# Up projection of a two-layer trunk: high weights times high and low activations as one 512-column product, halves added at eviction, and one ring of four PSUM banks

## The chip, the cores and the metric

The kernel runs on one core of a Trainium2 chip (trn2). The metric is device time in microseconds (us) from start to end of one execution. TensorE (PE) does the matrix products and writes them to PSUM, which has 8 banks of 128 partitions x 2 KB; VectorE (DVE), ScalarE (ACT) and GpSimd (POOL) work on tiles in SBUF and read or write PSUM; SyncE (SP) issues the transfers from HBM. Each engine works through its own program in order and waits on semaphores for the others.

## The reference

Two layers on x of 256 tokens x 1024 channels in fp32. Each layer is FFN, mixer, FFN, each with a norm before and a norm after; the mixer of layer 0 is a causal convolution of width 31, that of layer 1 an HGRN2 recurrence.

```python
def swiglu_ffn(x, w_in, w_out):                  # w_in 1024 x 5632, w_out 2816 x 1024
    gate, up = jnp.split(x @ w_in, 2, axis=-1)
    return (jax.nn.silu(gate) * up) @ w_out

for layer in range(2):
    g = norm_gains[layer]
    h = swiglu_ffn(rms_norm(x, g[0]), ffn_w_in[layer, 0], ffn_w_out[layer, 0])
    x = x + 0.5 * rms_norm(h, g[1])
    hn = rms_norm(x, g[2])
    m = conformer_conv_module(hn, ...) if layer == 0 else hgrn2_mixer(hn, ...)
    x = x + rms_norm(m, g[3])
    h = swiglu_ffn(rms_norm(x, g[4]), ffn_w_in[layer, 1], ffn_w_out[layer, 1])
    x = x + 0.5 * rms_norm(h, g[5])
```

The convolution module is: project to 2048 channels, `a * sigmoid(gate)`, depthwise convolution, layer norm, silu, project back. HGRN2 projects to queries q, forget gates f, values and output gates, and scans the tokens with a decaying state.

## The kernel before

**Precision.** Every fp32 operand of a large product is split into a high and a low part (`split`, L130 to L132: ACT casts to fp32r, DVE subtracts), and a product is three: high x high, high x low, low x high. The activations' parts are `xth` and `xtl`, [channel, token], made by `pre_norm` (PE transposes at L168, ACT L172, DVE L178).

**Weights.** `weight` streams 328 tiles of 512 KB through a ring of four raw tiles; high and low parts (`wh`, `wl`) have rings of ten.

**FFN** (`ffn`). The 2816 hidden channels are eleven chunks `c` of 256. Chunk 0 goes token-major by `project`, for which the activations are the stationary operand and the weights 512 moving columns (L242, L243, and for the low activations L246). The other ten go channel-major by `up_both` and `channels`: a call of `channels` makes gate and up of 128 hidden channels for all 256 tokens, with a 128x128 weight block stationary and 256 tokens moving, 3 products for each of 8 k, for gate and for up, 48 in all (L281, L282, L283), into the two halves of one PSUM bank. One DVE multiply by the tokens' scales brings it to SBUF (L286); ACT Sigmoid L334, two DVE multiplies and a `split` make the hidden parts, which `down` multiplies with `w_out` (`expand`, `mm3`, L135 to L137) into four accumulator banks (`acc`). There are 80 such calls in the four FFNs and 8 in HGRN.

**Conv mixer** (200 to 275 us). For each token tile t and chunk c: `gate` (a `project`, then DVE L396, ACT L399, DVE L401 and a split into `lg`), then `conv`: the products u from `lg` (a Fourier transform, L135 to L137 into a bank `tr`), DVE L421 to L425 and a split into `cc`, then the products v back, from `cc`. Eight (t, c) in all.

**HGRN scores** (711 to 790 us). For each half: `channels` calls for f and q, then `scores`: eight products L547, a multiply of q by f (L550), and seven levels in a chain: eight products L562 into a bank `tr` (each shows as two records in the trace), DVE `copy_predicated` L568 (a copy L565 in the last level), DVE multiply of q (L573), POOL L577 and L579; then X at L624.

**Between the parts.** `start` (L290 on) runs the `pre_norm` of tile 0, then `rest` of the part before (the last down products and `post_norm` of tile 1), then the `pre_norm` of tile 1. `post_norm` is ACT L212, DVE L213, POOL L146 and L148, DVE L218, which writes `x`.

**What sets the order.** The kernel is written in the order above; the framework that builds it places each engine's instructions by priority as their inputs and buffers come free, so that products of one step stand between those of another. The eight PSUM banks are three rings: `acc` 4, `mm` 2 (`project`, `channels`) and `tr` 2 (transposes, u, v, scores, X).

Of the kernel before, what the change touches and what calls it, by code (L numbers as in the profile page):

```python
# [8 lines left out]
F32 = mybir.dt.float32  # L9
F32R = mybir.dt.float32r  # L10
U8 = mybir.dt.uint8
AF = mybir.ActivationFunctionType
ALU = mybir.AluOpType
# [3 lines left out]
P = 128  # L17
D = 1024
ROOT = 32.0
KD = D // P  # L20
# [3 lines left out]
SEQ = 256  # L24
NT = SEQ // P
# [15 lines left out]
def trunk_kernel(  # L41
# [14 lines left out]
    act, dve, pool, pe = nc.scalar, nc.vector, nc.gpsimd, nc.tensor  # L56

    const = ctx.enter_context(tc.tile_pool(name="const", bufs=1))
    sb = ctx.enter_context(tc.tile_pool(name="sb", bufs=2))
    ps = ctx.enter_context(tc.tile_pool(name="ps", bufs=2, space=PSUM))  # L60
# [3 lines left out]
    def new(pl, shape, dtype, tag, bufs):  # L64
        count[0] += 1
        return pl.tile(shape, dtype, tag=tag, name=f"{tag}_{count[0]}", bufs=bufs)

    def b4(dtype=F32):
        return new(sb, [P, 1024], dtype, "b4", 10)

    def wide(tag, dtype=F32):
        return new(sb, [P, 512], dtype, tag, {"ga": 2, "lg": 5, "ca": 2, "cb": 2, "cc": 4}[tag])

    def narrow(tag, dtype=F32):
        return new(sb, [P, 256], dtype, tag, {"e": 4, "hid": 4}[tag])

    def tiny(n=1):
        return new(sb, [P, 16], F32, "tiny", 16)[:, :n]
# [1 line left out]
    def acc():  # L80
        return new(ps, [P, 512], F32, "acc", 4)

    def mm():
        return new(ps, [P, 512], F32, "mm", 2)

    def tr():
        return new(ps, [P, 512], F32, "tr", 2)

    ident = const.tile([P, P], F32, name="ident")
    make_identity(nc, ident)  # L90
# [5 lines left out]
    pool.memset(ones, 1.0)  # L96

    xs = [const.tile([P, D], F32, name=f"x{t}") for t in range(NT)]
    xth = const.tile([P, NT * D], F32R, name="xth")
    xtl = const.tile([P, NT * D], F32R, name="xtl")  # L100
    xkh = xth.rearrange("p (t k m) -> p k t m", t=NT, m=P)
    xkl = xtl.rearrange("p (t k m) -> p k t m", t=NT, m=P)
    gcol = const.tile([P, G_END], F32, name="gcol")
    nc.sync.dma_start(xs[0][:, :512], x_in[0, :P, :512])
    nc.sync.dma_start(gcol, cols)
# [54 lines left out]

    def pre_norm(t, gi):
        src = xs[t]
        hi, lo = xth[:, t * D : (t + 1) * D], xtl[:, t * D : (t + 1) * D]
        for h in range(2):
            pt = tr()
            for j in range(4):
                k = h * 4 + j
                pe.transpose(pt[:, j * P : (j + 1) * P], src[:, k * P : (k + 1) * P], ident)  # L168
            for j in range(4):
                k = h * 4 + j  # L170
                g = gcol[:, gi * KD + k : gi * KD + k + 1]
                last_hi[0] = act.activation(hi[:, k * P : (k + 1) * P],  # L172
                                            pt[:, j * P : (j + 1) * P], AF.Copy, scale=g).ins
            for j in range(4):
                k = h * 4 + j
                g = gcol[:, gi * KD + k : gi * KD + k + 1]
                sl = slice(k * P, (k + 1) * P)
                dve.scalar_tensor_tensor(  # L178
                    lo[:, sl], pt[:, j * P : (j + 1) * P], g, hi[:, sl].bitcast(F32),
                    op0=ALU.mult, op1=ALU.subtract,  # L180
                )
        if gi == 0:
            return hi, lo, None
        return hi, lo, mean_square(src)
# [86 lines left out]
        return res  # L271

    def channels(ws, cols_, scales):
        o = mm()
        for part in range(2):
            og = o[:, part * SEQ : (part + 1) * SEQ]
            for k in range(KD):
                wh, wl = ws[k // 2]
                col = (k % 2) * 512 + cols_[part]
                cs = slice(col, col + P)  # L280
                pe.matmul(og, wh[:, cs], xkh[:, k], start=k == 0, stop=False)  # L281
                pe.matmul(og, wh[:, cs], xkl[:, k], start=False, stop=False)  # L282
                pe.matmul(og, wl[:, cs], xkh[:, k], start=False, stop=k == KD - 1)  # L283
        res = wide("ga")
        pair = lambda ap: ap.rearrange("p (g n) -> p g n", g=2)
        dve.tensor_tensor(pair(res), pair(o), scales.unsqueeze(1).broadcast_to([P, 2, SEQ]),  # L286
                          op=ALU.mult)
        return res

    def start(gi, before):  # L290
        first = pre_norm(0, gi)
# [87 lines left out]
    def conv_mixer(layer, spectrum, before):  # L379
# [4 lines left out]
        xt = start(base, before)  # L384
# [61 lines left out]
            return z  # L446

        def turn(t, z):
            hi, lo = xth[:, t * D : (t + 1) * D], xtl[:, t * D : (t + 1) * D]
            for h in range(2):  # L450
                pt = tr()
                for j in range(4):
                    k = h * 4 + j
                    pe.transpose(pt[:, j * P : (j + 1) * P], z[:, k * P : (k + 1) * P], ident)
                y, s = hc[t][:, h * 512 : (h + 1) * 512], z[:, h * 512 : (h + 1) * 512]
                for j in range(4):
                    k = h * 4 + j
                    js = slice(j * P, (j + 1) * P)
                    g = gcol[:, G_LN + k : G_LN + k + 1]
                    b = gcol[:, G_LN + KD + k : G_LN + KD + k + 1]  # L460
                    act.activation(y[:, js], pt[:, js], AF.Identity, scale=g, bias=b)
                step = 256 if h == 0 else 512
                for a in range(0, 512, step):
                    bs = slice(a, a + step)
                    act.activation(s[:, bs], y[:, bs], AF.Sigmoid)
                    dve.tensor_tensor(y[:, bs], y[:, bs], s[:, bs], op=ALU.mult)
                    sl = slice(h * 512 + a, h * 512 + a + step)
                    split(hi[:, sl], lo[:, sl], y[:, bs])
            return hi, lo
# [27 lines left out]
    def hgrn_mixer(layer, lower, before):  # L497
        lb, omlb, gn, msk = lower
        base = layer * 3 + 1
        xt = start(base, before)  # L500
# [38 lines left out]
        def scores(f, k, q):  # L539
            s = b4()  # L540
            grid = lambda ap: ap.rearrange("p (g t) -> p g t", t=P)
            for pr in range(2):
                pt = tr()
                sl = slice(pr * 512, (pr + 1) * 512)
                for j in range(4):
                    js = slice(pr * 512 + j * P, pr * 512 + (j + 1) * P)
                    pe.matmul(pt[:, j * P : (j + 1) * P], k[:, js], q[:, js], start=True, stop=True)  # L547
                dve.tensor_tensor(grid(s[:, sl]), grid(pt),
                                  ident.unsqueeze(1).broadcast_to([P, 4, P]), op=ALU.mult)
            dve.tensor_tensor(q, q, f, op=ALU.mult)  # L550
            tot = f
            for i, m in enumerate(LEVELS):
                nb = 1024 // (2 * m)
                per = P // (2 * m)
                qv = q.rearrange("p (b two m) -> p b two m", two=2, m=m)
                kv = k.rearrange("p (b two m) -> p b two m", two=2, m=m)
                sv = s.rearrange("p (b two m) -> p b two m", two=2, m=m)
                tv = tot.rearrange("p (b two) -> p b two", two=2)
                pt = tr()
                rows_ = 64 if m == 64 else P  # L560
                for g in range(8):
                    pe.matmul(pt[:rows_, g * 64 : (g + 1) * 64], k[:, g * P : g * P + rows_],  # L562
                              qv[:, g * per : (g + 1) * per, 1, :], start=True, stop=True)
                if m == 64:
                    dve.tensor_copy(sv[:64, :, 1, :],  # L565
                                    pt[:64].rearrange("p (b m) -> p b m", m=m))
                else:
                    dve.copy_predicated(  # L568
                        sv[:, :, 1, :],
                        msk[:, i, :].rearrange("p (b m) -> p b m", m=m),  # L570
                        pt.rearrange("p (b m) -> p b m", m=m),
                    )
                dve.tensor_tensor(qv[:, :, 1, :], qv[:, :, 1, :],  # L573
                                  tv[:, :, 0:1].broadcast_to([P, nb, m]), op=ALU.mult)
                if m < 64:
                    nt = (wide("ca") if m == 1 else narrow("e"))[:, :nb]
                    pool.tensor_tensor(nt.unsqueeze(2), tv[:, :, 0:1], tv[:, :, 1:2], op=ALU.mult)  # L577
                    tot = nt
                pool.tensor_tensor(kv[:, :, 0, :], kv[:, :, 0, :],  # L579
                                   tv[:, :, 1:2].broadcast_to([P, nb, m]), op=ALU.mult)  # L580
            return s
# [33 lines left out]
        scales = token_scales(xt)  # L615
        cross = b4()
        for half in range(2):
            f, k = forget(half, [weight() for _ in range(4)])
# [3 lines left out]
            pt = tr()  # L622
# [220 lines left out]
```

## Time and profile before

| | before |
|---|---|
| median of 3 runs | 1032.33 us (1032.0 to 1032.75) |
| profiled execution | 1030.74 us |
| its span in the trace | 1029.0 us (1.74 us lie outside it) |
| PE busy | 1004.7 us, 98% of the span |
| weight loads, beside it | 913.2 us, 89% |
| DVE busy | 705.6 us, 69% |
| ACT busy | 504.7 us, 49% |
| POOL busy | 71.0 us, 7% |
| granted TensorE clock, mean | 0.996 |
| HBM read | 179 MB, 175 GB/s over the span |

Busy time of PE counts the modelled end of each product, so neighbouring products overlap in it: the time that a product costs in a row of products is the distance between starts, not its duration. DVE's and ACT's durations overlap a little in the same way.

### The profile page before, as it was taken

Reading aid. Unit: us, or ns where it says so; the run is one execution under the profiler, and the core shown is the slowest. Engines: PE = TensorE matmul, PEld = TensorE weight load, DVE = VectorE, ACT = ScalarE, POOL = GpSimd, SP = SyncE. Lnnn points to the kernel's source line nnn. Section 1 sums busy time; section 2 is a strip of 40 time slices with the busy share of each in tenths; the row PEclk is TensorE's granted clock in tenths of the full one; section 3 lists DMA queues with packets and bytes.
Section 4 is the critical chain, followed back from the end, with each engine's and each line's share of the span. In section 5 each row is a group of like instructions: output and inputs, shape, how many; then the busy total and the mean of one; then the engine's idle time right before and its main releaser. Section 6 shows DMA issues by size and latency. Waiting matters only on the chain. (4 is left out here: it accounts for less than half of the span.)

```text
span 1029.0 us, 16850 instructions
## 1 busy us (share of the span) xinstructions
PE 1004.7 (98%) x6676; PEld 913.2 (89%) x6676; DVE 705.6 (69%) x1092; ACT 504.7 (49%) x852; POOL 71.0 (7%) x116
## 2 busy tenths in 40 slices
PE   7999999999899999999999999999999999999997
PEld 6999999888779999998899999989888879999996
DVE  6766666899887565658675656677676586666663
ACT  7544444764485444446544444574143473444441
POOL 1000000000010000000100000021343020000000
PEclk9999999999999999999999999999999999999999
DMA  7756464843536465647464646555222555564641
GB/s 254 259 198 212 156 211 142 270 164 111 182 101 226 168 199 170 223 152 241 144 206 163 205 164 226 185 202 179 87 84 91 176 175 186 161 215 155 215 143 41
DMA packets 50510, 181.14 MB, mean 176 GB/s; under 512 B 5985, under 2 KB 6113, under 8 KB 50432
## 3 DMA queue, kind: packets, MB, share of 16 engines
q1 hardware_dynamic: 50432, 180.07, 52.6%
q8 instruction: 52, 0.85, 0.3%
q14 instruction: 26, 0.21, 0.1%
HBM read 179.00 MB, written 1.05 MB: 175 GB/s over the span
## 5 line engine op out<-in xcount | busy, mean ns | idle before, releaser
L132 DVE TENSOR_TENSOR wl<-raw,wh 128x1024 fp32r<-128x1024 f32 (+1 forms) x386 | 400.6, 1059 | 200.4 <-ACT wh L131 196.8
L131 ACT CAST wh<-raw 128x1024 fp32r<-128x1024 f32 (+1 forms) x386 | 336.5, 923 | 275.4 <-PE mm L282 127.5
L281 PE MATMUL mm<-xth,wh 128*128 128x256 f32 x1408 | 396.3, 281 | 0.0
L282 PE MATMUL mm<-xtl,wh 128*128 128x256 f32 x1408 | 396.3, 281 | 0.0
L283 PE MATMUL mm<-xth,wl 128*128 128x256 f32 x1408 | 396.0, 281 | 0.0
L281 PEld LDWEIGHTS mm<-xth,wh 128*128 128x128 f32 x1408 | 265.8, 189 | 3.2 <-DVE e L335 0.7
L282 PEld LDWEIGHTS mm<-xtl,wh 128*128 128x128 f32 x1408 | 265.1, 188 | 2.6
L283 PEld LDWEIGHTS mm<-xth,wl 128*128 128x128 f32 x1408 | 266.1, 189 | 0.5 <-DVE wl L132 0.2
L136 PE MATMUL acc<-wl,b 128*128 128x512 f32 x352 | 137.8, 391 | 0.0
L137 PE MATMUL acc<-wh,b 128*128 128x512 f32 x352 | 137.7, 391 | 0.0
L135 PE MATMUL acc<-wh,b 128*128 128x512 f32 x352 | 137.6, 391 | 0.0
L137 PEld LDWEIGHTS acc<-wh,b 128*128 128x128 f32 x352 | 66.1, 188 | 14.1
L135 PEld LDWEIGHTS acc<-wh,b 128*128 128x128 f32 x352 | 66.1, 188 | 11.5
L136 PEld LDWEIGHTS acc<-wl,b 128*128 128x128 f32 x352 | 66.1, 188 | 11.4
L334 ACT ACTIVATE e<-ga 128x256 f32<-128x256 f32 x80 | 33.4, 418 | 79.8 <-DVE ga L286 79.8
L242 PE MATMUL mm<-wh,xth 128*128 128x512 f32 x176 | 70.7, 401 | 0.0
L243 PE MATMUL mm<-wl,xth 128*128 128x512 f32 x176 | 70.1, 398 | 0.0
L286 DVE TENSOR_TENSOR ga<-mm,scales 128x512 f32<-128x512 f32 x88 | 60.2, 685 | 12.4 <-PE mm L283 12.2
L146 POOL TENSOR_SCALAR tiny<-tiny 128x1 f32<-128x1 f32 (+1 forms) x30 | 8.4, 281 | 802.6 <-ACT b L212 711.5
L131 ACT CAST b<-e 128x256 fp32r<-128x256 f32 x80 | 32.4, 405 | 53.2 <-DVE e L336 53.2
L246 PE MATMUL mm<-wh,xtl 128*128 128x512 f32 x176 | 49.8, 397 | 0.0
L132 DVE TENSOR_TENSOR b<-e,b 128x256 fp32r<-128x256 f32 x80 | 33.8, 422 | 21.3 <-ACT b L131 21.3
(156 smaller groups left out, 877.4 us busy)
## 6 DMA issues: line engine op xcount, KB each, us to landing
raw<-wts SPq DMA_DIRECT2D x328, 512.0 KB, 5.0
b<-rows SPq DMA_DIRECT2D x10, 512.0 KB, 6.1
out_dram<-x SPq DMA_DIRECT2D x4, 256.0 KB, 2.1
x<-x_in SPq DMA_DIRECT2D x2, 256.0 KB, 2.8
x<-x_in SPq DMA_DIRECT2D x1, 512.0 KB, 4.2
b<-dft SPq DMA_DIRECT2D x1, 371.0 KB, 4.6
ca<-masks SPq DMA_DIRECT2D x1, 192.0 KB, 4.8
b<-w_dw SPq DMA_DIRECT2D x1, 124.0 KB
```

The source lines that it names most:

```text
L131: last_split[0] = act.copy(dst_h, src).ins
L132: dve.tensor_tensor(dst_l, src, dst_h.bitcast(F32), op=ALU.subtract)
L135: pe.matmul(o, lh, rh, start=first, stop=False)
L136: pe.matmul(o, lh, rl, start=False, stop=False)
L137: pe.matmul(o, ll, rh, start=False, stop=last)
L242: pe.matmul(o, hi[:, kp], wh[:, sl], start=k == 0, stop=False)
L243: pe.matmul(o, hi[:, kp], wl[:, sl], start=False, stop=False)
L246: pe.matmul(o, a, w, start=False, stop=h == 1 and n == 3)
L281: pe.matmul(og, wh[:, cs], xkh[:, k], start=k == 0, stop=False)
L282: pe.matmul(og, wh[:, cs], xkl[:, k], start=False, stop=False)
L283: pe.matmul(og, wl[:, cs], xkh[:, k], start=False, stop=k == KD - 1)
L286: dve.tensor_tensor(pair(res), pair(o), scales.unsqueeze(1).broadcast_to([P, 2, SEQ]), op=ALU.mult)
```

## The change

`channels` makes two products for each k in place of three. The high weights meet the high and the low activations in one product of 512 columns, which lie side by side in one tile `xt`; the low weights meet the high activations in one of 256, added onto the first half. Gate and up have a bank each. The second half of the bank (high weights x low activations) is copied to SBUF by ACT, DVE adds the first half to it, and when both parts are there one DVE multiply applies the scales, from SBUF. The banks are `acc` 4 and one ring `mm` of 4, `tr` being another name for it; the level products of `scores` take their banks from `acc`. The ring `e` of SBUF tiles grows from 4 to 6.

```diff
     def narrow(tag, dtype=F32):
-        return new(sb, [P, 256], dtype, tag, {"e": 4, "hid": 4}[tag])
+        return new(sb, [P, 256], dtype, tag, {"e": 6, "hid": 4}[tag])
...
     def mm():
-        return new(ps, [P, 512], F32, "mm", 2)
-
-    def tr():
-        return new(ps, [P, 512], F32, "tr", 2)
+        return new(ps, [P, 512], F32, "mm", 4)
+
+    tr = mm
...
-    xth = const.tile([P, NT * D], F32R, name="xth")
-    xtl = const.tile([P, NT * D], F32R, name="xtl")
-    xkh = xth.rearrange("p (t k m) -> p k t m", t=NT, m=P)
-    xkl = xtl.rearrange("p (t k m) -> p k t m", t=NT, m=P)
+    xt_all = const.tile([P, NT * 2 * D], F32R, name="xt")
+    xhl = xt_all.rearrange("p (t s k m) -> p k s t m", t=NT, s=2, m=P)
+
+    def turned(t):
+        return [xt_all[:, (2 * t + s) * D : (2 * t + s + 1) * D] for s in range(2)]
...
     def channels(ws, cols_, scales):
-        o = mm()
+        both = wide("ga")
         for part in range(2):
-            og = o[:, part * SEQ : (part + 1) * SEQ]
+            o = mm()
+            pair = o.rearrange("p (s t m) -> p s t m", s=2, m=P)
             for k in range(KD):
                 wh, wl = ws[k // 2]
                 col = (k % 2) * 512 + cols_[part]
                 cs = slice(col, col + P)
-                pe.matmul(og, wh[:, cs], xkh[:, k], start=k == 0, stop=False)
-                pe.matmul(og, wh[:, cs], xkl[:, k], start=False, stop=False)
-                pe.matmul(og, wl[:, cs], xkh[:, k], start=False, stop=k == KD - 1)
-        res = wide("ga")
-        pair = lambda ap: ap.rearrange("p (g n) -> p g n", g=2)
-        dve.tensor_tensor(pair(res), pair(o), scales.unsqueeze(1).broadcast_to([P, 2, SEQ]),
-                          op=ALU.mult)
-        return res
+                pe.matmul(pair, wh[:, cs], xhl[:, k], start=k == 0, stop=False)
+                pe.matmul(pair[:, 0], wl[:, cs], xhl[:, k, 0], start=False, stop=k == KD - 1)
+            cross = narrow("e")
+            act.copy(cross, o[:, SEQ:])
+            dve.tensor_tensor(both[:, part * SEQ : (part + 1) * SEQ], o[:, :SEQ], cross, op=ALU.add)
+        grp = both.rearrange("p (g n) -> p g n", g=2)
+        dve.tensor_tensor(grp, grp, scales.unsqueeze(1).broadcast_to([P, 2, SEQ]), op=ALU.mult)
+        return both
...
         def scores(f, k, q):
             for pr in range(2):
-                pt = tr()
+                pt = acc()
...
             for i, m in enumerate(LEVELS):
-                pt = tr()
+                pt = acc()
```

With the rings, the order of the built program changes, in places that the diff doesn't touch. Three of them follow, all on PE, before first and then after. In the names, the number behind a tile tells one use of its buffer from another.

**Conv mixer.** `lg` is what u is made from, `cc` what v is made from; L242, L243 and L246 are products of a `project`. Before, in the middle of a `project` (mm_2516):

```order
L246 MATMUL mm_2516<-wh_2433,xtl 128x512
L135 MATMUL tr_2414<-cc_2410,b_157_1008 128x256
L246 MATMUL mm_2516<-wh_2433,xtl 128x512
L242 MATMUL mm_2516<-wh_2441,xth 128x512
L243 MATMUL mm_2516<-wl_2442,xth 128x512
L136 MATMUL tr_2414<-cc_2411,b_157_1008 128x256
L137 MATMUL tr_2414<-cc_2410,b_158_1009 128x256
L135 MATMUL tr_2414<-cc_2410,b_157_1008 128x256
L136 MATMUL tr_2414<-cc_2411,b_157_1008 128x256
L137 MATMUL tr_2414<-cc_2410,b_158_1009 128x256
L135 MATMUL tr_2489<-lg_2486,b_157_1008 81x256
L242 MATMUL mm_2516<-wh_2441,xth 128x512
```

After, first the end of the `project` whose result becomes lg_2206, with the first two of the twelve products of u behind it; then the last product of that u, and what follows it up to the next `project` (mm_2274):

```order
L246 MATMUL mm_2175<-wh_2108,xt 128x512 x2
L135 MATMUL mm_2209<-lg_2206,b_181_935 81x256
L136 MATMUL mm_2209<-lg_2206,b_181_935 81x256
```

```order
L137 MATMUL mm_2209<-lg_2145,b_182_936 81x256
L135 MATMUL mm_2233<-cc_2229,b_181_935 128x256
L242 MATMUL mm_2274<-wh_2244,xt 128x512
L243 MATMUL mm_2274<-wl_2245,xt 128x512
L242 MATMUL mm_2274<-wh_2244,xt 128x512
L136 MATMUL mm_2233<-cc_2230,b_181_935 128x256
```

Before, u and v (tr) of earlier tiles stand among the products of a later `project`. After, u stands right behind the `project` that it is made from, and v's first product right behind the last of the same tile's u.

**HGRN scores.** Before, around two successive levels of the first half:

```order
L562 MATMUL tr_7653<-b_1236_7532,b_1219_7393 128x64 x8
L282 MATMUL mm_7781<-xtl,wh_7775 128x256
L283 MATMUL mm_7781<-xth,wl_7776 128x256
L281 MATMUL mm_7838<-xth,wh_7757 128x256
L282 MATMUL mm_7838<-xtl,wh_7757 128x256
...
L281 MATMUL mm_7838<-xth,wh_7763 128x256
L282 MATMUL mm_7838<-xtl,wh_7763 128x256
L562 MATMUL tr_7667<-b_1236_7532,b_1219_7393 128x64 x8
```

After, the whole `scores` of the first half, from q's last product to the first of the next `channels`:

```order
L283 MATMUL mm_7039<-xt,wl_6970 128x256
L548 MATMUL acc_7063<-b_1422_6973,b_1399_6852 128x128 x4
L548 MATMUL acc_7069<-b_1422_6973,b_1399_6852 128x128 x4
L563 MATMUL acc_7076<-b_1422_6973,b_1399_6852 128x64 x8
L563 MATMUL acc_7090<-b_1422_6973,b_1399_6852 128x64 x8
L563 MATMUL acc_7104<-b_1422_6973,b_1399_6852 128x64 x8
L563 MATMUL acc_7118<-b_1422_6973,b_1399_6852 128x64 x8
L563 MATMUL acc_7132<-b_1422_6973,b_1399_6852 128x64 x8
L563 MATMUL acc_7146<-b_1422_6973,b_1399_6852 128x64 x8
L563 MATMUL acc_7160<-b_1422_6973,b_1399_6852 64x64 x8
L625 MATMUL mm_7172<-b_1422_6973,b_1399_6852 128x128 x4
L282 MATMUL mm_7205<-xt,wh_7180 128x512
```

Before, products of `channels` stand between the levels; after, the levels and X stand together with nothing between.

**Start of a part.** `x_76` is the residual of tile 1. Before, near the end of a part's first `project` (mm_5311):

```order
L243 MATMUL mm_5311<-wl_5282,xth 128x512
L168 MATMUL tr_5227<-ident,x_76 128x128 x4
L242 MATMUL mm_5311<-wh_5289,xth 128x512
L168 MATMUL tr_5240<-ident,x_76 128x128 x4
L243 MATMUL mm_5311<-wl_5290,xth 128x512
```

After, at the same place (L137 is the last of the down products of the part before):

```order
L137 MATMUL acc_3352<-wh_4641,b_954_4645 128x512
L168 MATMUL mm_4866<-ident,x_76 128x128 x4
L168 MATMUL mm_4879<-ident,x_76 128x128 x4
L242 MATMUL mm_4950<-wh_4904,xt 128x512
L243 MATMUL mm_4950<-wl_4905,xt 128x512
```

Before, tile 1's transposes stand late in tile 0's `project`; after, they stand ahead of it. All five starts behind the kernel's first have this order.

## Rows read from the trace of the kernel before

**Rows 1.** The page, part 1: busy time, share of the span, instructions.
```profile
PE 1004.7 (98%) x6676; PEld 913.2 (89%) x6676; DVE 705.6 (69%) x1092; ACT 504.7 (49%) x852; POOL 71.0 (7%) x116
```
**Rows 2.** Windows: us, PE, PEld, DVE, ACT, POOL busy (x), PEclk, DMA share, GB/s.
```profile
200.00:255.00 55.00, 54.28 (x279) 44.92 (x280) 51.32 (x112) 30.26 (x74) 3.20 (x8) 1.00 0.46 159
305.00:480.00 175.00, 175.00 (x1232) 164.18 (x1231) 115.09 (x164) 82.18 (x119) 2.16 (x5) 1.00 0.59 197
711.00:790.00 79.00, 75.48 (x565) 68.27 (x563) 60.16 (x78) 22.03 (x28) 29.11 (x25) 1.00 0.32 107
```
**Rows 3.** Timeline of PE: start us, us, engine, line, out<-in, xcount [idle before].
```profile
904.78 0.40 PE L135 MATMUL acc<-wh,b 128*128 128x512 f32 x1
...
907.52 0.28 PE L281 MATMUL mm<-xth,wh 128*128 128x256 f32 x1
...
913.22 0.40 PE L135 MATMUL acc<-wh,b 128*128 128x512 f32 x1
```
**Rows 4.** The page, part 5: groups, busy, mean ns | idle before, releaser.
```profile
L334 ACT ACTIVATE e<-ga 128x256 f32<-128x256 f32 x80 | 33.4, 418 | 79.8 <-DVE ga L286 79.8
L286 DVE TENSOR_TENSOR ga<-mm,scales 128x512 f32<-128x512 f32 x88 | 60.2, 685 | 12.4 <-PE mm L283 12.2
```
**Rows 5.** Timeline of PE in the conv mixer, around the first products of a u.
```profile
216.00 0.28 PE L135 MATMUL tr<-lg,b 128*81 128x256 f32 x1
216.12 0.40 PE L243 MATMUL mm<-wl,xth 128*128 128x512 f32 x1
```
**Rows 6.** Groups of DVE, shapes apart, 200 to 290 us.
```profile
L396 DVE SCALAR_TENSOR_TENSOR ga<-mm,tiny,b 128x512 f32<-128x512 f32 x8 | 6.0, 745 | 0.1
...
L421 DVE TENSOR_TENSOR ca<-tr,b 81x512 f32<-81x512 f32 x8 | 5.5, 682 | 1.1 <-PE tr L137 1.1
...
L132 DVE TENSOR_TENSOR lg<-e,lg 128x256 fp32r<-128x256 f32 x8 | 3.3, 417 | 0.0
...
L422 DVE TENSOR_TENSOR cb<-tr,b 81x256 f32<-81x256 f32 x8 | 3.3, 410 | 0.0
```
**Rows 7.** Groups of ACT, shapes apart, 200 to 290 us.
```profile
L131 ACT CAST cc<-ca 81x512 fp32r<-81x512 f32 x8 | 4.9, 615 | 10.1 <-DVE ca L425 10.1
...
L131 ACT CAST lg<-e 128x256 fp32r<-128x256 f32 x8 | 3.2, 405 | 2.2 <-DVE e L401 2.2
```
**Rows 8.** Timeline of PE, 258 to 286 us: the conv mixer's end.
```profile
265.35 0.39 PE L135 MATMUL tr<-cc,b 81*128 81x256 f32 x1 [2.77 <-ACT cc L131]
```
**Rows 9.** Timeline of DVE in the HGRN scores of the first half.
```profile
717.90 1.22 DVE L550 TENSOR_TENSOR b<-b,b 128x1024 f32<-128x1024 f32 x1
721.26 1.37 DVE L568 COPY_PREDICATED b<-msk,tr 128x512 f32<-128x512 uint8 x1 [2.15 <-PE tr L562]
722.41 1.03 DVE L573 TENSOR_TENSOR b<-b,b 128x512 f32<-128x512 f32 x1
...
741.48 0.73 DVE L568 COPY_PREDICATED b<-msk,tr 128x512 f32<-128x512 uint8 x1
742.11 1.06 DVE L573 TENSOR_TENSOR b<-b,e 128x512 f32<-128x512 f32 x1
```
**Rows 10.** Timeline of PE in the same stretch: the products of the second level.
```profile
723.59 1.97 PE L562 MATMUL tr<-b,b 128*128 128x64 f32 x16 [0.76 <-DVE b L573]
```
**Rows 11.** Timeline of all engines at the end of a part, 486 to 495 us.
```profile
487.66 0.39 PE L242 MATMUL mm<-wh,xth 128*128 128x512 f32 x1
...
489.30 0.40 PE L243 MATMUL mm<-wl,xth 128*128 128x512 f32 x1
...
490.28 1.40 DVE L218 SCALAR_TENSOR_TENSOR x<-b,tiny,x 128x512 f32<-128x512 f32 x2
```
**Rows 12.** Windows after the wait of Rows 8.
```profile
265.00:268.00 3.00, 1.90 (x11) 1.47 (x12) 3.00 (x7) 2.49 (x8) 0.00 (x0) 0.85 0.15 61
268.00:270.00 2.00, 2.00 (x11) 2.00 (x11) 2.00 (x6) 1.91 (x7) 0.00 (x0) 0.50 0.76 248
270.00:272.00 2.00, 2.00 (x12) 1.82 (x12) 1.35 (x4) 2.00 (x6) 0.00 (x0) 0.87 0.62 203
```

More of the change, by code (lines that the diff above doesn't have):

```diff
@@ L162, in pre_norm @@
         src = xs[t]
-        hi, lo = xth[:, t * D : (t + 1) * D], xtl[:, t * D : (t + 1) * D]
+        hi, lo = turned(t)
         for h in range(2):
@@ L448, in turn @@
         def turn(t, z):
-            hi, lo = xth[:, t * D : (t + 1) * D], xtl[:, t * D : (t + 1) * D]
+            hi, lo = turned(t)
             for h in range(2):
```

## Prediction

> **What bounds the kernel now.** The page's first part comes first: PE is busy for 98% of the span, no other engine for more than 69% [rows 1]. A share over the whole span hides the stages, so windows come next [rows 2]: in the steady FFN PE has no idle time at all (175.00 us of 175.00, at full granted clock); in the conv mixer 54.28 of 55, in the HGRN scores 75.48 of 79. PE's program is the bound everywhere, and it is gapless because waits of one step are filled with products of another. So two things have to be priced: what a product costs in a row of products, and whether the fill is still there.
>
> **The product itself.** 48 products of 256 columns lie between the starts at 907.52 and 913.22: 5.70 us, 118.75 ns each. Twelve of 512 columns lie between 904.78 and 907.52: 2.74 us, 228 ns each [rows 3]. In `project`, seven products of 512 from 487.66 to 489.30 take 234 ns each [rows 11]. The change replaces high x high and high x low (2 x 118.75 = 237.5 ns) by one product of 512 columns (228 to 234 ns): a gain of 3.5 to 9.5 ns. There are 88 calls x 2 parts x 8 = 1408 such pairs, so 5 to 13 us; I take 230 ns, which gives **-11 us**. The columns are what is paid for, not the count of products, so merging two saves little.
>
> The Trainium skill, "TensorE: Matmul & The Clock Gate", section "Back-to-back issue gap", gives a sustained spacing of about 131 ns for 512 columns. The rows above show 228, so the measurement decides; by the page the pair would save 106 ns, 150 us in all. A product whose weight load sets its price is a rival below.
>
> **The eviction.** For each call one DVE multiply from PSUM (685 ns) becomes two ACT copies of 256 columns (like the 418 ns of L334), two DVE adds (0.42, as other 256-column operations of DVE) and one multiply from SBUF (no row has its like; between 417 for 256 columns [rows 6] and the 685 from PSUM, taken near the latter: 650) [rows 4]. On the chain from the last product to the hidden parts that is 0.42 + 0.42 + 0.65 - 0.69 = +0.8 us for the later part; the earlier part is evicted during the later one's products. In the FFN the products that use a call's result stand at least one block of `down` or one call away, 2.7 and 5.7 us of products each, and ACT and DVE carry 82 and 115 us of those 175 [rows 2]; the 20 calls of an FFN add some 17 us to ACT and 16 to DVE. So the added work is covered, at nothing in the steady state; if the cover were gone it would cost 0.8 x 80 = 64 us, which I hold out by the zero idle time now. At each of four FFN starts one short wait shows in the new order (a `down` right behind the transposes of its hidden part: an ACT cast, 0.41 us, with about 0.25 for the hand-over): 2.6 us. FFN ends and the first FFN I put at 2.5 us. **+5 us.**
>
> **The order, conv mixer.** This is the large term, and the diff doesn't show it. Now u and v of one tile stand inside the `project` of another, a product of u 0.12 us ahead of one of L243 [rows 5]. After, u stands right behind its own `project`, and v right behind its own u. PE must then wait out two chains in each of the eight (t, c), with nothing else to do. Chain A, from the last product to u: 0.16 (end of a product behind its start's spacing) + 0.745 (L396) + 0.418 (ACT L399, as L334) + 0.417 (DVE L401, as the other 256-column operation) + 0.405 (cast) = 2.14, with some 0.25 for hand-overs, and u's second product waits about 0.3 more for the low part (0.417 less one product) [rows 4, 6, 7]: 2.7 us. Chain B, from u's end to v: 0.16 + 0.682 (L421) + four of 0.41 (L422 to L425) + 0.615 (cast) = 3.1 us [rows 6, 7]. The trace has chain B once, where nothing was left to fill it: PE waits 2.77 us for the cast of `cc` at 265.35 [rows 8]. So 5.7 us for each of seven tiles, 40; on about three of them weight casts stand between on ACT or DVE, 2 more in sum; the last tile keeps some cover, 1.9. **+44 us.** Bounds: 8 x (2.3 + 2.6) = 39 below, and 8 x 6.8 = 54 if weight casts of 0.6 to 0.7 us get into both chains each time.
>
> **The order, HGRN scores.** Before, products of `channels` fill the seven levels; after, the levels and X stand back to back. A level's DVE part, `copy_predicated` and multiply, lasts from 721.26 to 723.44 (2.18 us) in the first level and from 741.48 to 743.17 (1.69) in the sixth [rows 9]; PE starts 0.15 us behind [rows 10]. The seven links sum to 12.4 (a mean of 1.77), with 0.3 each for hand-overs 14.5 us in which PE has nothing. Ahead of them PE waits for q (eviction, Sigmoid and a multiply of 512 columns, each 0.65 to 0.69, behind two short ones of 0.42: about 3.3 us with hand-overs) and for q times f (a 512-column multiply at 0.69, L550 at 1.22: about 2.1) [rows 9]. So 20 us in the first half and 19 in the second, less the 3.5 us that the window waits now [rows 2] (up to 5.8 by the spacing of starts). **+33 us.** Bounds: without the q chain 27; with every link as long as the first, 14 x 0.41 more, 39.
>
> **The order, starts.** At five starts the transposes of tile 1's `x` now stand ahead of tile 0's first `project`, which covered `post_norm` until now. PE comes free at 487.66, and `x` is complete only at 490.28 + 1.40 = 491.68 [rows 11]; transposing its first half can begin at about 491.0, so some 3.6 us of each start are idle. Five times 3.6 is 18, the mixer's bias adds put 1 on top, and waits of 1.3 that are there today go. **+18 us.** Bounds 14 and 22.
>
> **The clock.** After the wait that ends at 265.35 the granted clock fell: 0.85, then 0.50 from 268 to 270, then 0.87 [rows 12]. 0.50 is the lower of the two levels, 1.2 GHz against 2.4. In sum about 3.4 us ran at the half level, which costs 1.7 us. The changed kernel has such a wait some 12 times (seven tiles and five starts): 12 x 1.7 = 20. In the scores PE would be idle for most of 20 us twice; the windows of before don't show such a stretch. Half clock throughout would put some 13 us on each half, 26 together; none is the other end, and I take 13. **+33 us**, from 0 to 60.
>
> **Sum.** -11 + 5 + 44 + 33 + 18 = 89 us at full clock, and 33 for the clock: +122. Against the profiled execution (1030.74: a span of 1029.0 and 1.74 outside it) that is 1153; the median of the runs lies 1.6 us above it: **1154 us**. Against the sum's large terms the intended gain of 11 us is small.
>
> **Rivals.**
> The clock holds its upper level in spite of the waits: 1030.7 + 89 + 1.6 = 1121. For it: the mean granted clock of before is 0.996, and windows with small waits [rows 2] show 1.00. Against it: the one wait of that length which the trace has was followed by the fall [rows 12]. Chance 0.25.
>
> The clock stays low longer: half throughout the scores, and twice as long after each tile's and start's wait. 26 + 12 x 2.7 = 58: 1179. For it: in the conv mixer one wait follows the other after 6 us of products or less, so there is less time to recover than at 270. Chance 0.13.
>
> The waits are half covered: the framework's order is fixed, but chain A or the q chain may start earlier, since ACT and DVE would be less crowded while PE idles. Half of the conv and scores terms with their clock: 1154 - 38 - 15 = 1101. Against it: the chains were worked out from durations alone, which idle neighbours don't shorten. Chance 0.06.
>
> The other side: the wide product is paid by its weight load, not by its columns, so that 512 columns cost hardly more than 256 with one load less. The weight loads are 89% of the span beside PE's 98% [rows 1], and the 256-column spacing of 118.75 ns [rows 3] would then be the load's. With 118.75 for the wide product too the gain is 1408 x 118.75 = 167 us instead of 11, and the time is 1154 - 156 = 998. To be faster than before it needs a gain of over 133 us, a wide product below 143 ns. Against it: products of 512 columns with a weight load of the same size each run at 228 [rows 3], and here too each has its own load. Chance 0.03.
>
> The change doing nothing that can be measured (cover complete, -11 + 5, 1026) would need PE to run its program out of order; 0.01. The forecast itself: 0.52.
>
> **How the numbers follow.** A measurement of this kernel can tell about 0.2%, 2 us, from no change. Only the last two cases lie below 1030: faster 0.04, same 0.01, slower 0.95. The range: the forecast with the bounds of its terms, ordered by chance, from just below the full-clock rival to just above the slow-clock one, leaves out the half-covered case, the other side and the ends of the rest: 1112 to 1185.
>
> **What would show it.** Pairs of `channels` in the steady FFN should take 228 to 234 + 119 ns, a call 5.5 to 5.65 us, with PE as gapless there as before. In the conv mixer PE should wait about 2.5 us for ACT's `lg` and 3 us for `cc`, once each for each tile; in the scores some 2 us for DVE ahead of each level; at each start some 3.6 us ahead of L168. The granted clock should show 0.5 stretches behind these. The forecast is wrong if PE's waits sum to less than 80 us, if windows of waiting stay at 1.00, or if the wide product is below 200 ns.

## The result, and the profile after

The changed kernel takes 1177.89 us (median of 4 runs, 1175.04 to 1178.06), the kernel before 1032.54 beside it: a ratio of 1.1402, 95% interval 1.1385 to 1.1419. The forecast was 1154 with a range of 1112 to 1185. The time lies in the range, 24 us above the forecast.

The page of the profiled execution, span, part 1 (busy time, share, instructions) and the clock row of part 2 (40 equal slices, tenths of full speed):

```profile
span 1176.2 us, 14551 instructions
...
PE 1056.1 (90%) x5268; PEld 891.0 (76%) x5268; DVE 775.1 (66%) x1268; ACT 557.8 (47%) x1028; POOL 71.1 (6%) x116
...
PEclk9999999767788999999999999995675999999999
```

Against [rows 1] PE's busy time rose by 51.4 us (1056.1 less 1004.7), although it executes 1408 products fewer, and its idle time rose by 95.8 (120.1 less 24.3). The clock row shows two dips, one in the conv mixer and one in the HGRN part. Cut at the first transposes L168 of each part, the last part up to its last product, the trace shows where the time went:

| part (its start included) | before, us | after, us | difference |
|---|---|---|---|
| first FFN | 197.3 | 199.4 | +2.1 |
| conv mixer | 89.6 | 154.6 | +65.0 |
| second FFN | 193.2 | 198.8 | +5.6 |
| third FFN | 188.6 | 192.2 | +3.6 |
| HGRN | 153.4 | 219.0 | +65.6 |
| last FFN | 197.3 | 202.5 | +5.2 |

A second cut goes by kinds. Take the distance between the starts of successive products, and price each product at the spacing it has in gapless rows at full clock (230 ns for 512 columns, 119 for 256, 111 below). An excess of up to the price again is a product at the lower clock; a longer one is a wait. So parted, the span is:

| | before, us | after, us | difference |
|---|---|---|---|
| products at full clock | 992.8 | 981.5 | -11.3 |
| excess by the clock | 12.9 | 57.1 | +44.2 |
| waits | 20.2 | 132.9 | +112.7 |
| scatter about the prices, ends | 3.1 | 4.7 | +1.6 |

The border between the second and third kind is not sharp: a wait taken so holds the end of the product ahead of it, and at the lower clock its slow half too. That is why the waits rise by 112.7 us here and PE's idle time by 95.8. The sum is the span.

**Where nothing is lost.** Windows of the steady FFN, columns as in [rows 2]:

```profile
60.00:200.00 140.00, 140.00 (x743) 118.95 (x742) 106.14 (x175) 78.17 (x133) 0.00 (x0) 1.00 0.57 189
...
390.00:555.00 165.00, 165.00 (x875) 141.52 (x874) 120.29 (x187) 87.78 (x149) 0.44 (x2) 1.00 0.56 187
```

PE has no gap there, as in [rows 2]: the longer eviction is hidden. Its three steps, from part 5 of the page, columns as in [rows 4]:

```profile
L286 DVE TENSOR_TENSOR ga<-mm,e 128x256 f32<-128x256 f32 x176 | 71.6, 420 | 77.6 <-ACT e L285 77.2
L285 ACT COPY e<-mm 128x256 f32<-128x256 f32 x176 | 64.6, 368 | 95.1 <-PE mm L283 95.0
...
L288 DVE TENSOR_TENSOR ga<-ga,scales 128x512 f32<-128x512 f32 x88 | 61.1, 695 | 1.4
```

The timeline of PE in that stretch gives the price of the pair:

```profile
399.70 0.39 PE L282 MATMUL mm<-xt,wh 128*128 128x512 f32 x1
399.93 0.28 PE L283 MATMUL mm<-xt,wl 128*128 128x256 f32 x1
400.05 0.39 PE L282 MATMUL mm<-xt,wh 128*128 128x512 f32 x1
```

230 and 120 ns from start to start, against three times 118.75 [rows 3]. The 131 ns that the Trainium skill ("TensorE: Matmul & The Clock Gate", "Back-to-back issue gap") gives for 512 columns isn't seen here either.

**The conv mixer.** Timeline of PE through one tile; the brackets give idle time and its releaser:

```profile
217.95 1.09 PE L246 MATMUL mm<-wh,xt 128*128 128x512 f32 x4
221.23 0.50 PE L135 MATMUL mm<-lg,b 128*81 128x256 f32 x1 [2.19 <-ACT lg L131]
...
222.63 0.41 PE L137 MATMUL mm<-lg,b 128*81 128x256 f32 x1
225.93 0.58 PE L135 MATMUL mm<-cc,b 81*128 81x256 f32 x1 [2.88 <-ACT cc L131]
226.30 0.63 PE L242 MATMUL mm<-wh,xt 128*128 128x512 f32 x1
226.73 0.63 PE L243 MATMUL mm<-wl,xt 128*128 128x512 f32 x1
```

Both chains stand open: 2.19 us for `lg` and 2.88 for `cc`, the second as in [rows 8]. The products behind them start 0.43 us apart in place of 0.23: the lower level of the clock. The products of u stand at it already (0.41 us in place of 0.28), and it lasts until 231, some five us of products behind the second wait.

**The scores.** Timeline of PE up to the first level, then of all engines through one level:

```profile
797.78 1.97 PE L548 MATMUL acc<-b,b 128*128 128x128 f32 x8 [3.71 <-DVE b L528]
801.67 3.68 PE L563 MATMUL acc<-b,b 128*128 128x64 f32 x16 [1.92 <-DVE b L551]
```

```profile
807.62 3.64 PE L563 MATMUL acc<-b,b 128*128 128x64 f32 x16 [2.28 <-DVE b L574]
811.30 1.29 DVE L569 COPY_PREDICATED b<-msk,acc 128x512 f32<-128x512 uint8 x1 [3.83 <-PE acc L563]
811.41 1.29 POOL L580 TENSOR_TENSOR b<-b,ca 128x512 f32<-128x512 f32 x1 [4.49 <-PE acc L563]
812.39 0.85 DVE L574 TENSOR_TENSOR b<-b,ca 128x512 f32<-128x512 f32 x1
813.36 3.49 PEld L563 LDWEIGHTS acc<-b,b 128*128 128x128 f32 x16 [2.29 <-POOL b L580]
813.39 3.65 PE L563 MATMUL acc<-b,b 128*128 128x64 f32 x16 [2.13 <-DVE b L574]
```

PE first waits 3.71 us for q and 1.92 for q times f. The level shown then takes 5.77 us: the same eight products that took 1.97 us in [rows 10] now take 3.65, and then PE waits 2.13 for the link. Windows of the two stretches of scores, and of a piece of the second:

```profile
793.00:842.00 49.00, 28.95 (x139) 27.33 (x138) 20.01 (x24) 2.81 (x5) 9.24 (x7) 0.55 0.13 43
866.00:912.00 46.00, 28.23 (x135) 26.67 (x134) 19.80 (x24) 2.60 (x4) 8.46 (x7) 0.54 0.13 46
875.00:900.00 25.00, 16.68 (x76) 16.04 (x76) 7.59 (x8) 0.00 (x0) 5.03 (x4) 0.50 0.00 2
```

The clock is at its lower level (0.50) through the levels; it does not come back between one wait and the next.

**The starts.** Timeline of PE at the end of the second FFN:

```profile
564.02 1.29 PE L168 MATMUL mm<-ident,x 128*128 128x128 f32 x8 [3.35 <-DVE x L218]
```

That is the wait for `post_norm` which [rows 11] let foresee. By the spacings it is 3.5 us; the four others last 3.9 to 4.9.

### The profile page after: what moved, and what is told of

It is laid out like the page before. It is cut to its first block, busy times and chain, and to the rows that moved or that the text cites. A ratio compares the mean times of both kernels' runs of the same rounds, so it can differ in the third digit from the quotient of the medians.

```text
span 1176.2 us, 14551 instructions
## 1 busy us (share of the span) xinstructions
PE 1056.1 (90%) x5268; PEld 891.0 (76%) x5268; DVE 775.1 (66%) x1268; ACT 557.8 (47%) x1028; POOL 71.1 (6%) x116
## 5 line engine op out<-in xcount | busy, mean ns | idle before, releaser
L282 PE MATMUL mm<-xt,wh 128*128 128x512 f32 x1408 | 495.0, 394 | 0.0
L283 PE MATMUL mm<-xt,wl 128*128 128x256 f32 x1408 | 394.3, 280 | 0.0
L282 PEld LDWEIGHTS mm<-xt,wh 128*128 128x128 f32 x1408 | 265.4, 189 | 59.1 <-DVE ga L288 0.5
L283 PEld LDWEIGHTS mm<-xt,wl 128*128 128x128 f32 x1408 | 265.7, 189 | 3.0 <-DVE wl L132 0.2
L137 PE MATMUL acc<-wh,b 128*128 128x512 f32 x352 | 139.1, 396 | 0.4 <-DVE b L132 0.2
L286 DVE TENSOR_TENSOR ga<-mm,e 128x256 f32<-128x256 f32 x176 | 71.6, 420 | 77.6 <-ACT e L285 77.2
L285 ACT COPY e<-mm 128x256 f32<-128x256 f32 x176 | 64.6, 368 | 95.1 <-PE mm L283 95.0
L137 PEld LDWEIGHTS acc<-wh,b 128*128 128x128 f32 x352 | 66.2, 188 | 18.0 <-DVE b L132 4.1
L242 PE MATMUL mm<-wh,xt 128*128 128x512 f32 x176 | 79.5, 452 | 0.0
L243 PE MATMUL mm<-wl,xt 128*128 128x512 f32 x176 | 77.6, 441 | 0.0
L136 PEld LDWEIGHTS acc<-wl,b 128*128 128x128 f32 x352 | 66.4, 189 | 11.3
L563 PE MATMUL acc<-b,b 128*128 128x64 f32 (+1 forms) x224 | 47.7, 406 | 28.1 <-DVE b L574 24.3
L288 DVE TENSOR_TENSOR ga<-ga,scales 128x512 f32<-128x512 f32 x88 | 61.1, 695 | 1.4
```

The source lines that it names most:

```text
L136: pe.matmul(o, lh, rl, start=False, stop=False)
L137: pe.matmul(o, ll, rh, start=False, stop=last)
L242: pe.matmul(o, hi[:, kp], wh[:, sl], start=k == 0, stop=False)
L243: pe.matmul(o, hi[:, kp], wl[:, sl], start=False, stop=False)
L282: pe.matmul(pair, wh[:, cs], xhl[:, k], start=k == 0, stop=False)
L283: pe.matmul(pair[:, 0], wl[:, cs], xhl[:, k, 0], start=False, stop=k == KD - 1)
```

## The experiments

The theory after these readings: the ring alone makes the loss, by the order in which it has the program built; by the table above some five parts of it are waits and two are the lower clock, which the waits bring with them. The rivals: the wide product or the two-step eviction is at fault; or the clock falls for some other reason.

### The rings of before, with the wide product

The last two lines of the edit stand for both places in `scores`.

```diff
     def mm():
-        return new(ps, [P, 512], F32, "mm", 4)
-
-    tr = mm
+        return new(ps, [P, 512], F32, "mm", 2)
+
+    def tr():
+        return new(ps, [P, 512], F32, "tr", 2)
...
-                pt = acc()
+                pt = tr()
```

> The changed kernel with the two rings of before (mm 2, tr 2; scores take their banks from tr again); the wide product, the eviction in halves and the ring e of 6 stay. In the built order u, v, the levels of scores and the transposes stand among other products again, as before. My theory (the ring alone makes the loss, by the order): PE's waits in the conv mixer, the scores and the starts go, the granted clock is back at 0.99 or more, the wide product gives its 11 us, and with two banks for two parts PE may wait a little for an eviction: 1021 to 1035 us. Rival (the loss comes from the wide product or the two-step eviction): 1100 us or more.

Measured: 1028.09 us, ratio to the kernel before 0.9949 (0.9932 to 0.9965). Its page and, of its windows, one of the steady FFN and one of the scores:

```profile
span 1027.6 us, 14523 instructions
...
PE 995.7 (97%) x5268; PEld 844.2 (82%) x5268; DVE 770.7 (75%) x1268; ACT 557.0 (54%) x1028; POOL 68.6 (7%) x116
```

```profile
60.00:200.00 140.00, 139.89 (x742) 118.88 (x741) 105.52 (x174) 78.10 (x133) 0.00 (x0) 1.00 0.56 187
...
715.00:790.00 75.00, 68.64 (x452) 59.48 (x451) 57.30 (x80) 21.44 (x32) 23.65 (x23) 1.00 0.27 96
```

Waits are 28.9 us (before 20.2), the excess by the clock 15.6. The wide product and its eviction stay in this kernel, and the loss is gone: the ring is the cause. It is about 5 us (0.5%) faster than the kernel before, less than the 11 us that its products save: in the profiled executions the second, third and last FFN are shorter by 2.8, 2.4 and 2.8 us, the first FFN, conv mixer and HGRN longer by 1.7, 3.3 and 1.6.

### The ring alone

The kernel before with `mm` of 4, `tr = mm`, and the two banks of `scores` from `acc` (the last two lines stand for both); products and eviction are the old ones.

```diff
     def mm():
-        return new(ps, [P, 512], F32, "mm", 2)
-
-    def tr():
-        return new(ps, [P, 512], F32, "tr", 2)
+        return new(ps, [P, 512], F32, "mm", 4)
+
+    tr = mm
...
-                pt = tr()
+                pt = acc()
```

> The kernel before with the ring alone changed (mm 4, tr the same ring, levels of scores from acc); three products of 256 columns and one DVE multiply as before. My theory: the order is the changed kernel's, so are its waits, and the 11 us of the wide product are missing: 1189 us (1180 to 1195), idle time of PE in the conv mixer and scores as in the changed kernel. Rival (wide product or eviction make the loss): 1032 us.

Measured: 1183.92 us (1.1464, 1.1443 to 1.1484). Of its timeline of PE, a u and a v of the conv mixer (lines are one or two lower in this kernel):

```profile
219.96 0.34 PE L134 MATMUL mm<-lg,b 128*81 128x256 f32 x1 [2.19 <-ACT lg L130]
...
224.16 0.58 PE L134 MATMUL mm<-cc,b 81*128 81x256 f32 x1 [2.88 <-ACT cc L130]
```

The same two waits, to the hundredth, without a single wide product. It lies 6 us above the changed kernel and not 11; by the spacings its products cost 11.3 more, its waits 4.4 and its clock 2.3 less. Together with the run before it this settles the cause from both sides.

### One term at a time: the conv mixer

```diff
-            u = tr()
+            u = acc()
...
-            v = tr()
+            v = acc()
```

> The changed kernel with u and v of the conv mixer in banks of acc; nothing else is changed, and in the built order only the conv mixer has u and v among the products of other projects again. My theory: the conv mixer's part of the trace (154.6 us from its first transposes to those of the next FFN) goes back to about 100, since its start still waits; the other parts stay: 1123 us (1115 to 1130). Rival (the waits come from too few buffers or slower evictions, not from the order): within 5 us of 1178.

Measured: 1120.20 us (1.0834). The conv mixer's part is 99.1 us in place of 154.6; every other part is within 1.6 us of the changed kernel. So the open u and v with their share of the clock cost 55 us, by the spacings of that part 40 for waits and 15 for the clock. The forecast had 44 for their waits and some 12 to 14 for their clock.

### One term at a time: the scores

One line: the bank of X.

```diff
             X[half] = cross[:, half * 512 : (half + 1) * 512]
-            pt = tr()
+            pt = acc()
```

> The changed kernel with one line changed: X, behind the last level of the scores, takes its bank from acc in place of the shared ring. In the built order the levels then stand among channels products again. My theory: X alone held the next channels back, by its place in the ring; the HGRN part goes from 219 us to about 165 (its start still waits), the others stay: 1124 us (1116 to 1130). Rival (the levels stand together because they are in acc, or for lack of other buffers): within 5 us of 1178.

Measured: 1124.65 us (1.0877). The HGRN part is 168.2 us in place of 219.0, by the spacings 33 us less of waits and 16 less of the clock; 15 us more than before the change remain, among them the wait of its start. Timeline of PE at the first product of the scores:

```profile
790.73 0.28 PE L283 MATMUL mm<-xt,wl 128*128 128x256 f32 x1
790.85 1.05 PE L548 MATMUL acc<-b,b 128*128 128x128 f32 x8
791.66 0.48 PE L282 MATMUL mm<-xt,wh 128*128 128x512 f32 x1
```

Products of `channels` follow at once. One tile in the ring, asked for behind a long chain, had held back everything that asks for a bank of that ring later in the code; the levels themselves had been in `acc` all the time.

### Three terms at once

u, v, X and the transposes of `pre_norm` in banks of `acc`:

```diff
     def pre_norm(t, gi):
         src = xs[t]
         hi, lo = turned(t)
         for h in range(2):
-            pt = tr()
+            pt = acc()
```

> The changed kernel, wide product and ring of 4, but u and v of the conv mixer, X of the scores and the transposes of pre_norm take their banks from acc, which is free there. The built order has u, v, levels and transposes among other products again. My theory: three of the four sums of waits go, what stays are the waits at the FFN starts (about 1.3 us each) and the first FFN (3 us): 1025 to 1036 us. Rival (the ring is not the cause): above 1120 us.

Measured: 1052.61 us (1.0211, 1.0176 to 1.0246), 17 us above the expected range. The rival is out, but the expectation missed. Timeline of PE, at the conv mixer's end, at the start behind it and at the one behind HGRN:

```profile
275.92 0.58 PE L135 MATMUL acc<-cc,b 81*128 81x256 f32 x1 [4.57 <-ACT cc L131]
...
295.46 1.78 PE L168 MATMUL acc<-ident,x 128*128 128x128 f32 x8 [3.58 <-DVE x L218]
```

```profile
842.31 1.97 PE L168 MATMUL acc<-ident,x 128*128 128x128 f32 x8 [2.63 <-DVE x L218]
```

Sharing `acc` makes the same fault in another place. In the code, `pre_norm` of tile 0 asks for its banks before the part before asks for the accumulators of its last products; with one ring, its transposes now stand ahead of these products and wait for `post_norm`. Three waits of about 1.3 us at FFN starts stay as well. So this run doesn't price the starts by themselves, and no other run changes them alone.

### Filling the waits

The changed kernel, with products in its waits that nobody reads; all its own work stays.

```diff
+    def fill(n):
+        o = acc()
+        for j in range(n):
+            with tc.issue_after(last_pe[0]):
+                product(o, xt_all[:, :P], xt_all[:, :512], start=j == 0, stop=j == n - 1)
...
             u = tr()
+            fill(8)
...
             v = tr()
+            fill(10)
...
             for i, m in enumerate(LEVELS):
+                fill(8)
```

(`fill(14)` ahead of the scores' first products and of tile 1's transposes at each start; `product` is `pe.matmul` that notes its instruction.)

> The changed kernel with products that nobody reads (512 columns, xt times xt, into an acc bank) placed in its waits: 8 ahead of each u, 10 ahead of each v, 14 ahead of the scores' first products, 8 ahead of each level, 14 ahead of tile 1's transposes at each start; at 0.23 us each they are shorter than the wait they stand in. My theory for the clock term (the granted clock falls because PE waits): the clock stays at 0.98 or more and the time falls by the part that products run slow, 44 us more than before by their spacings: 1125 to 1140 us. Rival (the clock falls for another reason, and these waits cost only themselves): the filling runs at half clock, 0.43 us each, outlasts the waits by about 1 us each, and the time rises to 1190 or more.

Measured: 1129.61 us (1.0939, 1.0920 to 1.0958), 48 us less than the changed kernel, with more to do. Its mean granted clock is 0.995 against 0.922. Timeline of PE through two levels (all products carry the helper's line):

```profile
782.54 2.10 PE L117 MATMUL acc<-xt 128*128 128x512 f32 x8
785.04 1.97 PE L117 MATMUL acc<-b,b 128*128 128x64 f32 x16 [0.40 <-DVE b L590]
786.82 2.10 PE L117 MATMUL acc<-xt 128*128 128x512 f32 x8
789.17 1.97 PE L117 MATMUL acc<-b,b 128*128 128x64 f32 x16 [0.26 <-DVE b L590]
```

The level products are back at 1.97 us, and a level takes 3.9 to 4.3 in place of 5.5 to 6.0. The clock falls because PE waits, and that part of the loss is worth at least 48 us (from the fourth level on no gap is left ahead of the products, so there the filling may last a little longer than the wait): 26 in the HGRN part (219.0 to 193.2), 15 in the conv mixer (154.6 to 139.7), the rest in the FFNs. The waits themselves stay, under the filling, and so does the rest of the loss.

### The wide product taken apart

The kernel with the rings of before, with two products of 256 for each wide one; the high x low ones stand behind the others, so that each half of the bank is a closed sum.

```diff
             for k in range(KD):
-                pe.matmul(pair, wh[:, cs], xhl[:, k], start=k == 0, stop=False)
+                pe.matmul(pair[:, 0], wh[:, cs], xhl[:, k, 0], start=k == 0, stop=False)
                 pe.matmul(pair[:, 0], wl[:, cs], xhl[:, k, 0], start=False, stop=k == KD - 1)
+            for k in range(KD):
...
+                pe.matmul(pair[:, 1], wh[:, cs], xhl[:, k, 1], start=k == 0, stop=k == KD - 1)
```

> The kernel with the rings of before and the eviction in halves (1028 us), but each product of 512 columns taken apart into two of 256, high x high and low x high first and high x low behind them, into the same halves of the bank. My theory: merging two products saves 237.5 less 230 ns for each of 1408 pairs, so taking them apart costs 11 us: 1039 us (1035 to 1044). Rival (the wide product saves nothing and the 1028 come from the eviction or the banks): 1028.

Measured: 1051.74 us (1.0179, 1.0157 to 1.0201), 24 us above the wide form and not 11. Timeline of PE in the steady FFN:

```profile
399.84 1.11 PE L289 MATMUL mm<-xt,wh 128*128 128x256 f32 x8
400.79 0.40 PE L136 MATMUL acc<-wh,b 128*128 128x512 f32 x1
```

Eight products in 0.95 us, 118.75 ns each: the price of the products is as stated, 11.3 us of the 21 us by which the profiled spans differ (1048.6 less 1027.6). Waits are 7 us more (35.9 against 28.9), of them some 2.4 in one wait of the conv mixer's end, and the scatter accounts for 2. Why so many small waits came in is not settled: taking products apart also moved the order in other places, so this run doesn't measure the merge alone. What the rows show of it are the 11.3 us of the products; with its eviction the wide form was 6 us ahead of the narrow one with the ring of four, and about 5 with two rings.

### Separate rings of 3 and 1, and u and v in acc besides

Against the first kernel of this section, the one with the rings of before:

```diff
-        return new(ps, [P, 512], F32, "mm", 2)
+        return new(ps, [P, 512], F32, "mm", 3)
...
-        return new(ps, [P, 512], F32, "tr", 2)
+        return new(ps, [P, 512], F32, "tr", 1)
```

> The changed kernel with a ring of 3 banks for project and channels and one bank of its own for transposes, u, v, scores and X. The built order has the interleaving. My theory: separate rings matter, not their sizes; the third bank takes away what waits channels had for an eviction, the single tr bank adds some in the conv mixer, where v must wait for the eviction of the u before: 1022 to 1036 us. Rival (a single tr bank strings u, v and levels together again): above 1050.

Measured: 1030.81 us (0.9973, 0.9961 to 0.9984). A ring of its own for the serial chains is what matters, down to a single bank. The conv mixer is 97.4 us here (92.9 with two banks). With u and v in `acc` on top (the edit of the conv mixer's experiment above):

> The changed kernel with a ring of 3 banks for project and channels, one bank for transposes, levels and X, and u and v of the conv mixer in banks of acc, which are free there. With the single bank for u and v the conv mixer's part took 97.4 us against 92.9 with two and 89.6 in the kernel before; the HGRN part and the first FFN were the shortest of all. My theory: four free banks for u and v give the conv mixer some 5 to 7 us back: 1022 to 1028 us. Rival (the conv mixer's end waits for the serial chains of its last tiles whatever the banks): 1029 to 1033.

Measured: 1031.02 us (0.9972, 0.9960 to 0.9985): the rival. The conv mixer's part fell to 93.8 us, but a wait stays at its end, and the median did not move. Timeline of PE:

```profile
275.46 0.58 PE L136 MATMUL acc<-cc,b 81*128 81x256 f32 x1 [3.96 <-ACT cc L132]
```

The first kernel of this section once more:

> The kernel with the rings of before and the wide product once more, beside the one above: 1028 us, 0.995 of the kernel before. If its gain was a matter of the chip, the ratio moves to 1.

Measured: 1028.61 us (0.9955, 0.9941 to 0.9969). The gain of the wide product with separate rings, about 0.5%, is there again. It is a repeat on the same chip, so it doesn't show whether another chip would give it. By the medians this is the fastest version found.

## Why the prediction was right, and where its size was off

**The product: right.** 230 ns were taken for the wide product, 230 are seen, and at these spacings the products' row gives -11.3 for the -11 of the sum.

**The eviction: right.** ACT's copy takes 368 ns and not 418, DVE's add 420, the multiply 695 (650 taken); the steady FFN is gapless. By the spacings the first FFN waits 0.7 us at its start, as taken (0.66), the three others 1.3.

**The order: right in place and mechanism, and near in size.** The waits were summed to 44 + 33 + 18 + 5 = 100 us. They rose by 113 by the spacings and by 96 as idle time of PE. In the conv mixer with its start it is 48 or 40 against 49, in HGRN with its start 43 or 37 against 37, in the four FFNs 22 or 18 against 14. In the scores the wait for q took 3.71 us by the row where 3.3 was taken, that for q times f 1.92 for 2.1, the seven links 1.9 to 2.3, 2.06 in the mean, for 2.07. POOL's multiply L580 was left out of the link; the rows above show it end half a us ahead of DVE's part, so between two levels it added nothing. At the starts the forecast's own readings, 487.66 and 491.0, give 3.3 us and not the 3.6 that it summed; the five waits were 3.5 to 4.9.

**The clock: the term that was mis-sized.** 33 us were taken, 48 is what the filling gave back (44 by the spacings). The conv mixer with its start was near: 8 x 1.7 = 14 taken, 15 given back. The scores were not. The forecast put 13 us on them, half way between nothing and the lower level throughout, for want of a row. Throughout is what the trace shows (0.50 from 875 to 900), and the 26 us of that bound are what the HGRN part, its start included, lost when filled. The trace of before held a hint: its one fall of the clock between start and end came after a single wait [rows 12], and in the scores a wait of 2 us follows every 2 us of products. Cut by parts, the forecast for HGRN comes to 33 + 13, 3.6 + 1.7 for its start and -1 for its products, 50 us, where 65.6 were measured: 15 of the 25 us by which the spans differ from the sum. Of the rest 7 lie in the FFNs and 3 in the conv mixer. The time lies in the upper part of the range, which was drawn to reach the rival with the slow clock.

**The rival with the lower clock for longer: half right, and its number is luck.** It gave 1179, and 1177.9 was measured. Its half about the scores is what happened. Its other half, twice as long after every other wait, is not: its 12 x 2.7 = 32 us stand against some 22 that the filling gave back outside HGRN (and twice 1.7 is 3.4, not 2.7, which would have made it 1187). Its clock term of 58 is above the 44 to 48 found, and the waits, larger by the spacings than summed, make up the difference. Still, a chance of 0.13 for the lower level throughout the scores was too small beside 0.52 for the middle value and 0.25 for no fall at all: a middle between two cases that were both named is not itself a case.

**The other rivals fell.** The clock at its upper level in spite of the waits (1121): 0.50 in the scores. Half covered waits (1101): 2.19 and 2.88 us in the conv mixer's rows, 3.71 for q. The wide product at its weight load's price (998): 230 ns.

## What to carry to other kernels

Price a change of buffers by the order of the built program, not by the lines of the diff: as this framework built it here, a ring of buffers shared between a serial chain and the work that covers it puts the chain's steps in the order of the code, and the cover is gone, while a ring of its own, even of one bank, keeps it. Merging two products that share a weight saves only a few ns (some 7 of 237 here) where the columns are what is paid for, so what the merged form needs elsewhere decides. A wait on TensorE in an otherwise gapless row costs more than its length, since the products behind it may run at half clock: here 48 us of a loss of 145.

## What the runs showed of the hardware

With a wait of about 2 us after every eight products of the scores the granted clock stayed at 0.50, the lower of its two levels, for 25 us and more, and a level's products that take 1.97 us took 3.65; in the conv mixer's first tile the lower level was there behind the wait of 2.2 us, and it ended some five us of products after the next, of 2.9. With useless products in the same waits it stayed at 0.995 in the mean, and the kernel was 4% faster for doing more.
